# Where attention's keys and queries lie on chip, and the queue of the first queries

## The chip, the cores and the metric

The kernel runs on one core of one Trainium2 chip, as a single program. The metric is the device time of one execution in microseconds (us), taken as the median over several executions. A core has a matrix engine (PE, with its weight loads shown apart as PEld), a vector engine (DVE), an activation engine (ACT), a general engine (POOL) and a sequencer for transfers (SP). Transfers between the large memory and the on-chip memory are issued by SP, ACT or POOL, each through a queue of its own, and all of them are carried by the same 16 DMA engines.

## The reference, cut to what matters

One step of a hybrid decoder layer, for a prompt of 2,048 tokens with 16 learned tokens in front (2,064 rows) and for 8 short samples of 4 tokens:

```python
q, k, v, u = project(rmsnorm(x), w_in)          # q, k, v: 4 heads of 128; u: 512 channels
att  = head_norm(diff_attention(q, k, v))       # two softmax maps a head, one taken from the other, causal
ssm  = glu(gelu(state_space_scan(u)))           # GLU: g * sigmoid(g @ w_glu + b)
x    = x + concat([att, ssm]) @ w_out
x    = x + w_down(gelu(conv3(rmsnorm(x) @ w_gate)) * (rmsnorm(x) @ w_up))
```

The samples attend to a paged cache of 2,048 past keys and values each, which the kernel gathers page by page.

## The kernel before, in words

The work is written stage by stage in `run`. A scheduler then orders the instructions of every engine by priority (the order of the text) and by the times of its own model of the chip; inside one engine the order is fixed from then on, and each instruction waits there for what it needs. On-chip buffers come from pools. A pool has tags, a tag has so many slots of equal size, and pools opened with `side="right"` are stacked downward from the top of the on-chip memory in the order in which they are opened. When a pool is closed its bytes can be taken by a later pool, and a tile of the later pool then waits for the last use of every earlier tile whose bytes it shares, and for nothing else (`reuse_waits="tile"`). A tile that a transfer reads counts as used until that transfer has ended.

The stages around the change, and what each holds on the right-hand side (bytes per partition, counted down from the top; sizes are summed from the tile shapes in the code):

- The state space layer. `ssc` (0 to 21,056) and `ssw` (21,056 to 83,328) hold its parameters and work tiles.
- The GLU (`glu`, L1077 and on) comes after it, in eight rounds. `glc` (0 to 16,416) holds its weights. `glw` (16,416 to 63,648) holds, from the far end: two small tiles to 61,088; `ghl` for the high part (61,088 to 56,224) and `ghl` for the low part (56,224 to 51,360), one buffer each; two `gT` (51,360 to 40,608); `gh` and `gl`, two each (40,608 to 19,104); two `sg` (19,104 to 16,416). A round loads `gT` from GT, splits it into `gh` and `gl`, multiplies with the weights, forms `sg` (L1112, L1113), splits that into `ghl` (L74, L75), and SP stores both `ghl` to the tensor ST (L1123).
- The projections of keys, queries and values (`project_kvq`) run beside the GLU. The transposed keys go to KST (L367, from SP), the queries to QST (L378, from ACT), both out of the tile `khl`; the values go to VST (L323, from ACT). The last chunk of tokens does keys, then queries, then values. The pool of these tiles is on the left-hand side and ends 84,864 below the top; its second `khl` buffer is the last thing in it.
- Attention (`attend`). For each of two halves of the queries and each head, `attend_head` loads two key tiles `kt` (c = 0 and 1, L431), value tiles `vt` (L435) and `v0` (L440). For each pair of query tiles (a group, numbered 3, 2, 1, 0, -1 in the first half), `attend_queries` loads `qs` by four transfers (L450), `attend_scores` multiplies, and `attend_values` sums the values. The first head's two key loads go through POOL's queue, all others and all query loads through SP's.

Attention's four pools are `atk` (four `kt` of 8,256 and three `qs` of 4,096: 45,312), `atw` (38,848: `vt`, `v0`, `e2`, `o2`, the small sums, `wT`, `oT`), `atc` (768) and `atp` (60,928: the weights `p`). Before, they are opened in the order `atk`, `atw`, `atc`, `atp`, so `atk` lies at 0 to 45,312, with the `kt` slots at its far end (slot 0 at 45,312 to 37,056, slot 3 at 20,544 to 12,288) and the `qs` slots at the very top.

After attention `out_attention` joins its result into x, and the samples' attention starts beside it. The pools of the latter are stacked from the top again: `smc` (0 to 6,784: page table `pgt`, the indices `idx` for the gathers, small constants) and `smw` (6,784 to 55,424: among them `qbd` at 47,104 to 38,400 and the gathered rows `kv` at 38,400 to 26,112). The page table is loaded (L596), 16 small DVE instructions make `idx` (L601, L602), and POOL gathers cache rows with them (L622), after it has cleared `qbd` (L633).

Of the kernel before, what the change touches and what calls it, by code (L numbers as in the profile page):

```python
# [10 lines left out]
F32 = mybir.dt.float32  # L11
# [49 lines left out]
class Step:  # L61
# [381 lines left out]
        o2 = wp.tile([P, NM + 1024], F32, name="o2", tag="o2", bufs=2)  # L443
        return {"h": h, "half": half, "e2": e2, "o2": o2, "q0": NM + 1024 if half else 0, "kt": kt, "vc": vc, "v0": v0}

    def load_queries(self, qs, h, q0, q1):

        for dup in range(2):
            for s in range(2):
                self.nc.sync.dma_start(out=qs[dup * 64 : dup * 64 + 64, s, :, : q1 - q0].bitcast(F32),  # L450
                                       in_=self.QST[s, h, :, :, q0:q1].rearrange("c d t -> d c t"))

    def attend_queries(self, grp, wp):
        h, g = grp["h"], grp["g"]
        q0 = NM + 256 * g if g >= 0 else 0
        q1 = NM + 256 * (g + 1)
        grp["q0"], grp["q1"] = q0, q1
        qs = grp["qs"] = wp.tile([P, 2, 2, 256], F32R, name="qs", tag="qs", bufs=QB)
        self.load_queries(qs, h, q0, q1)

    def attend_scores(self, grp, qi, wp, vp, ps):

# [1170 lines left out]
    def run(self):  # L1633
        tc = self.tc

        def pool(name, bufs, **kw):
            return tc.tile_pool(name=name, bufs=bufs, reuse_waits="tile", **kw)

        with ExitStack() as st:
            e = st.enter_context  # L1640
            cp = e(pool("const", 1))
            dp = e(tc.tile_pool(name="dram", bufs=1, space=DRAM))
            self.constants(cp)
            self.scratch(dp)
            with pool("psb", 2, space=PSUM) as pb:
                with ExitStack() as right:
                    with ExitStack() as left:
                        e = left.enter_context
                        pm = e(pool("pjm", 4, space=PSUM))
                        upa = ExitStack()  # L1650
                        pa = upa.enter_context(pool("psa", 2, space=PSUM))
                        xp = e(pool("xp", 1))
                        xq = e(pool("xq", 3))
                        wq = e(pool("pjw", 9))
                        sst = ExitStack()
                        sc = sst.enter_context(pool("ssc", 1, side="right"))

                        def params():
                            with pool("ssp", 1, side="right") as sp:
                                self.ssm_params(sc, sp, pb)  # L1660
                            with pool("ctmp", 1, side="right") as tp:
                                self.constants_later(tp)

                        with pool("pu", 2) as wu:
                            self.project_setup(xp, wu, pa)
                            kept = self.project_u(xq, wq, wu, pm, pa, params)
                        with pool("cvs", 1, side="right") as sp:
                            self.conv_setup(cp, sp, pb)
                        upa.close()
                        pa, pc = e(pool("psc", 1, space=PSUM)), e(pool("psd", 1, space=PSUM))  # L1670
                        wp = e(pool("pj", 2))
                        sw = sst.enter_context(pool("ssw", 1, side="right"))
                        self.first = self.tc.cur_priority
                        mats = [self.ssm_prepare(0, sw, pb)]
                        for bk in range(8):
                            Hh = self.ssm_states(bk, mats[bk], sw, pb)
                            if bk < 7:
                                mats.append(self.ssm_prepare(bk + 1, sw, pb))
                            self.ssm_outputs(bk, mats[bk], Hh, sw, pc)
                        self.ssm_finish(sw, pb)  # L1680
                        sst.close()
                        with pool("glc", 1, side="right") as gc, pool("glw", 2, side="right") as gw:
                            self.glu(gc, gw, pb)
                        self.project_kvq(kept, xq, wp, wq, pm, pa)
            with ExitStack() as fill:
                with ExitStack() as att:
                    e = att.enter_context
                    fil = e(pool("fil", 1, space=PSUM))
                    ps = e(pool("ats", 1, space=PSUM, side="right"))
                    pools = [e(pool(nm, n, side="right")) for nm, n in (("atk", 4), ("atw", 2), ("atc", 1), ("atp", 7))]  # L1690
                    self.attend(pools, ps)
                    with pool("osc", 1) as oc, pool("osw", 2) as ow:
                        self.out_ssm(oc, ow, fil)
                    oc = fill.enter_context(pool("oac", 1))
                    with pool("oaw", 1) as ow:
                        self.out_setup(oc, ow, 1)
                        self.out_attention(range(6), ow, fil)
                up = ExitStack()
                e = up.enter_context
                pb = e(pool("psf", 4, space=PSUM, side="right"))  # L1700
                sam = ExitStack()
                sc, sw = [sam.enter_context(pool(nm, n, side="right")) for nm, n in (("smc", 1), ("smw", 2))]
                with pool("oax", 2) as ow, pool("oap", 4, space=PSUM, side="right") as pa:
                    self.out_attention(range(6, 16), ow, pa, ahead=True)
            pg = up.enter_context(pool("fg", 4, space=PSUM, side="right"))
            fx, self.fr, self.fw, self.fz = [up.enter_context(pool(nm, 1)) for nm in ("fx", "fr", "fw", "fz")]
            self.up_setup(fx, pg, pb)
            self.sample_attention(sc, sw, pb)
            sam.close()
            with pool("obc", 1, side="right") as oc, pool("obw", 1, side="right") as ow:  # L1710
                self.out_setup(oc, ow, 2)
                self.out_attention([16], ow, pb)
            with pool("dw", 1, side="right") as wp:
                self.ffn_up()
                up.close()
                with pool("du", 1, side="right") as du, pool("dps", 1, space=PSUM) as pd, pool("da", 1) as da:
                    self.ffn_down(wp, da, du, pd)
# [59 lines left out]
```

## Time and profile before

| | us |
|---|---|
| median of 3 executions | 2915.77 |
| lowest, highest | 2908.78, 2924.84 |
| the profiled execution | 2908.63 |
| its span on the core | 2906.9 |
| PE busy | 2731.3 (94% of the span) |
| DVE busy | 2181.1 (75%) |
| ACT busy | 1505.3 (52%) |
| POOL busy | 830.7 (29%) |
| DMA, mean rate over the span | 176 GB/s |

The profile is of one execution. Busy time is the sum of an engine's instructions; idle time before an instruction carries the name of what ended it, and only idle time of the engine that sets the end costs anything. The granted clock of PE is given as a share of its full speed of 2.4 GHz (0.50 is its lower level, 1.2 GHz). A wait on several things is put down to the one that ended last by the profile, so the name can be that of something which merely ended near that moment.

### The profile page before, as it was taken

The page shows a single profiled execution, that of the slowest core. Times are in us where ns is not written, and L with a number is a line of the kernel's source. Part 1 is how long each engine was busy: PE and PEld are TensorE (multiplying, and loading weights), DVE is VectorE, ACT ScalarE, POOL GpSimd, SP SyncE. Part 2 cuts the span into 40 slices and gives each one's busy share as a digit, 9 for nine tenths or more (in the row PEclk, how much of TensorE's full clock was granted, in tenths as well). Part 3 has the DMA queues.
Part 4 walks back from the last instruction along what each step waited for, and adds up shares of the span by engine and source line. Part 5 has one row for each costly group of instructions (what it writes and reads, how often), then busy time and mean ns, then how long its engine had stood idle before and what let it go on. Part 6 is the DMA issues. An engine that isn't in the chain of part 4 may idle for free. (4 is left out here: it accounts for less than half of the span.)

```text
span 2906.9 us, 43475 instructions
## 1 busy us (share of the span) xinstructions
PE 2731.3 (94%) x14872; PEld 2359.9 (81%) x14872; DVE 2181.1 (75%) x4318; ACT 1505.3 (52%) x3051; POOL 830.7 (29%) x1272
## 2 busy tenths in 40 slices
PE   6899889989999999788999999999999999999999
PEld 6866668868887878667988998988998998787786
DVE  6748977756677888457888788888788995675565
ACT  5423334556667888236566556655555663222233
POOL 2525442112211232554343332342213442000000
PEclk9899999999999999899999999999999999999999
DMA  6676676787664442686455546454454437675562
GB/s 187 174 184 151 176 197 175 200 241 195 215 193 135 139 129 64 202 279 197 155 169 175 167 151 207 151 174 155 141 186 127 132 119 282 201 239 192 178 224 91
DMA packets 434614, 512.13 MB, mean 176 GB/s; under 512 B 91337, under 2 KB 339033, under 8 KB 433368
## 3 DMA queue, kind: packets, MB, share of 16 engines
q1 hardware_dynamic: 336520, 347.45, 41.6%
q0 software_dynamic: 23296, 82.81, 8.9%
q10 hardware_dynamic: 74576, 79.09, 8.2%
q8 instruction: 117, 1.92, 0.3%
q14 instruction: 105, 0.86, 0.1%
HBM read 381.32 MB, written 126.74 MB: 175 GB/s over the span
## 5 line engine op out<-in xcount | busy, mean ns | idle before, releaser
L80 PE MATMUL g<-xb,uw 128*128 128x384 f32 (+1 forms) x1848 | 596.3, 325 | 13.0 <-ACT uw L68 5.8
L81 PE MATMUL g<-xb,uw 128*128 128x384 f32 (+1 forms) x1848 | 595.3, 323 | 0.0
L82 PE MATMUL g<-xb,uw 128*128 128x384 f32 (+1 forms) x1848 | 583.0, 323 | 2.2 <-DVE uw L69 2.2
L80 PEld LDWEIGHTS g<-xb,uw 128*128 128x128 f32 x1848 | 347.6, 188 | 25.5 <-ACT uw L68 7.0
L81 PEld LDWEIGHTS g<-xb,uw 128*128 128x128 f32 x1848 | 348.1, 188 | 7.9 <-issue 2.3
L82 PEld LDWEIGHTS g<-xb,uw 128*128 128x128 f32 x1848 | 345.0, 188 | 9.3 <-DVE uw L69 3.5
L68 ACT ACTIVATE uw<-uraw 128x512 fp32r<-128x512 f32 x330 | 200.7, 625 | 122.3 <-PE g L82 74.5
L69 DVE TENSOR_TENSOR uw<-uraw,uw 128x512 fp32r<-128x512 f32 x330 | 241.6, 739 | 27.0 <-ACT uw L68 25.0
L491 ACT ACTIVATE p<-S,nms 128x484 f32<-128x484 f32 (+11 forms) x360 | 209.3, 590 | 63.3 <-DVE nms L490 50.5
L490 DVE TENSOR_REDUCE nms<-S 128x1 f32<-128x484 f32 (+11 forms) x360 | 191.5, 559 | 50.0 <-PE S L485 27.0
L80 PE MATMUL pq<-dw,da 128*128 128x512 f32 x528 | 209.7, 398 | 11.0 <-ACT da L68 7.3
L81 PE MATMUL pq<-dw,da 128*128 128x512 f32 x528 | 209.5, 397 | 0.0
L82 PE MATMUL pq<-dw,da 128*128 128x512 f32 x528 | 200.4, 395 | 6.2 <-DVE da L69 6.2
L68 ACT ACTIVATE da<-dt 128x1024 fp32r<-128x1024 f32 (+1 forms) x68 | 71.2, 1047 | 215.2 <-PE pq L82 146.6
L80 PE MATMUL pj<-wh,x 128*128 128x512 f32 (+1 forms) x408 | 168.7, 416 | 13.1 <-DVE wk L337 5.5
L81 PE MATMUL pj<-wl,x 128*128 128x512 f32 (+1 forms) x408 | 168.8, 414 | 3.8 <-DVE wl L75 3.8
L95 POOL TENSOR_TENSOR rs_y<-rs_v,half 128x8 f32<-128x8 f32 (+4 forms) x77 | 93.3, 1216 | 269.4 <-DVE rs_v L90 251.5
L82 PE MATMUL pj<-wh,x 128*128 128x512 f32 (+1 forms) x408 | 167.5, 411 | 0.0
L1322 POOL TENSOR_TENSOR uraw<-uraw 128x512 f32<-128x512 f32 x66 | 107.6, 1631 | 176.6 <-DVE s L1320 109.0
L484 PE MATMUL S<-kt,qs 128*128 128x484 f32 (+11 forms) x360 | 143.6, 401 | 8.4 <-DMA qs<-QST 5.3
L552 PE MATMUL O<-wT,vt 128*128 128x256 f32 x576 | 145.0, 388 | 2.6 <-ACT wT L547 2.1
L1449 DVE SCALAR_TENSOR_TENSOR z<-A,cw,z 128x768 f32<-128x768 f32 (+1 forms) x132 | 136.6, 1035 | 4.9 <-ACT z L1446 4.0
(434 smaller groups left out, 6867.4 us busy)
## 6 DMA issues: line engine op xcount, KB each, us to landing
dt<-MT SPq DMA_DIRECT2D x99, 512.0 KB
uraw<-in_w_gate_dram SPq DMA_DIRECT2D x66, 512.0 KB
uraw<-in_w_up_dram SPq DMA_DIRECT2D x66, 512.0 KB
raw<-in_w_in_dram SPq DMA_DIRECT2D x80, 256.0 KB
MT<-z ACTq DMA_DIRECT2D x44, 384.0 KB
qs<-QST SPq DMA_DIRECT2D x128, 128.0 KB
dT<-in_w_down_dram SPq DMA_DIRECT2D x44, 256.0 KB
draw<-in_w_down_dram POOLq DMA_DIRECT2D x44, 256.0 KB, 4.2
```

The lines of the kernel that those rows point to most:

```text
L68: nc.scalar.activation(hi, src, AF.Copy)
L69: nc.vector.tensor_tensor(out=lo, in0=src, in1=hi.bitcast(F32), op=ALU.subtract)
L80: mm(out, lhsT=lh, rhs=rh, start=start, stop=False, skip_group_check=goes_on)
L81: mm(out, lhsT=lh, rhs=rl, start=False, stop=False, skip_group_check=goes_on)
L82: mm(out, lhsT=ll, rhs=rh, start=False, stop=stop, skip_group_check=goes_on)
L95: nc.gpsimd.tensor_tensor(out=y, in0=v, in1=e, op=ALU.pow)
L484: nc.tensor.matmul(dst, lhsT=qs[:, 0, c, qa : qa + M], rhs=kt[c][:, x:y], start=True, stop=False)
L490: nc.vector.tensor_reduce(out=nms[:M, z : z + 1], in_=dst, axis=AX.X, op=ALU.max, negate=True)
L491: nc.scalar.activation(p[:M, Z + x : Z + y], dst, AF.Exp, bias=nms[:M, z : z + 1], accum_out=sms[:M, z : z + 1])
L552: nc.tensor.matmul(O[:, :N], lhsT=v, rhs=tw[:, m - a, :N], start=(m == 0), stop=(m == nb))
L1322: gp.tensor_tensor(out=a21, in0=a11, in1=a21, op=ALU.subtract)
L1449: nc.vector.scalar_tensor_tensor(out=z[:, :np_], in0=A[:, j : j + np_], scalar=cw[:, f, j : j + 1], in1=z[:, :np_], op0=ALU.mult, op1=ALU.add)
```

## The change

The pool with the keys and queries is opened third instead of first, so the four pools lie in the order `atw`, `atc`, `atk`, `atp`. Summed as above, `atw` is then at 0 to 38,848, `atc` at 38,848 to 39,616, and `atk` at 39,616 to 84,928: `qs` slots 2, 1, 0 at 39,616 to 43,712, 47,808 and 51,904, then `kt` slots 3, 2, 1, 0 at 51,904 to 60,160, 68,416, 76,672 and 84,928. `atp` stays where it was. Besides, the four query loads of head 0, group 3 (the first group of all) are issued by POOL instead of SP.

```diff
-    def load_queries(self, qs, h, q0, q1):
+    def load_queries(self, qs, h, q0, q1, eng):
         for dup in range(2):
             for s in range(2):
-                self.nc.sync.dma_start(out=qs[dup * 64 : dup * 64 + 64, s, :, : q1 - q0].bitcast(F32),
-                                       in_=self.QST[s, h, :, :, q0:q1].rearrange("c d t -> d c t"))
+                eng.dma_start(out=qs[dup * 64 : dup * 64 + 64, s, :, : q1 - q0].bitcast(F32),
+                              in_=self.QST[s, h, :, :, q0:q1].rearrange("c d t -> d c t"))
...
-        self.load_queries(qs, h, q0, q1)
+        self.load_queries(qs, h, q0, q1, self.nc.gpsimd if (h, g) == (0, 3) else self.nc.sync)
...
-                    pools = [e(pool(nm, n, side="right")) for nm, n in (("atk", 4), ("atw", 2), ("atc", 1), ("atp", 7))]
-                    self.attend(pools, ps)
+                    wp, cp_, kp, vp = [e(pool(nm, n, side="right")) for nm, n in (("atw", 2), ("atc", 1), ("atk", 4), ("atp", 7))]
+                    self.attend((kp, wp, cp_, vp), ps)
```

## Rows read from the trace of the kernel before

**Rows 1.** The page's first part: busy time, share of the span, instructions.
```profile
PE 2731.3 (94%) x14872; PEld 2359.9 (81%) x14872; DVE 2181.1 (75%) x4318; ACT 1505.3 (52%) x3051; POOL 830.7 (29%) x1272
```
**Rows 2.** Stretches: length, busy PE, PEld, DVE, ACT, POOL, clock, DMA share, GB/s.
```profile
624.00:664.00 40.00, 28.03 (x108) 19.42 (x107) 18.20 (x57) 20.48 (x58) 5.44 (x32) 0.79 1.08 290
636.00:640.00 4.00, 4.00 (x12) 2.63 (x12) 1.94 (x4) 2.47 (x6) 0.00 (x0) 0.55 1.03 289
654.00:664.00 10.00, 8.73 (x26) 6.34 (x27) 4.14 (x15) 4.50 (x13) 1.47 (x8) 0.52 1.14 237
...
1160.00:1200.00 40.00, 27.34 (x134) 22.50 (x133) 18.78 (x52) 14.56 (x36) 17.63 (x21) 0.79 0.53 147
1200.00:1350.00 150.00, 119.45 (x581) 98.53 (x579) 91.88 (x145) 62.83 (x113) 81.09 (x83) 0.92 0.83 263
1350.00:2425.00 1075.00, 1059.43 (x6451) 992.71 (x6452) 935.98 (x1534) 632.78 (x1102) 367.58 (x419) 1.00 0.50 156
```
**Rows 3.** PE in time order: start, length, instruction, idle before it and its releaser.
```profile
635.79 1.86 PE L484 MATMUL S<-kt,qs 128*128 128x456 f32 x4 [5.27 <-DMA qs<-QST]
...
654.84 0.77 PE L80 MATMUL po<-owh,sa 128*128 128x512 f32 x1 [3.98 <-DMA sa<-ST]
```
**Rows 4.** SP's issues in time order around the end of the projections.
```profile
608.54 2.73 SPq L1123 DMA_DIRECT2D ST<-ghl  x2
...
623.87 0.36 SPq L1123 DMA_DIRECT2D ST<-ghl  x1
...
627.63 2.45 SPq L450 DMA_DIRECT2D qs<-QST  x3
...
631.61 0.58 SPq L450 DMA_DIRECT2D qs<-QST  x1
```
**Rows 5.** POOL's issues of the first two key tiles.
```profile
622.85 0.75 POOL L431 DMA_DIRECT2D kt<-KST  x1 [20.57 <-DMA VST<-v]
624.40 0.54 POOL L431 DMA_DIRECT2D kt<-KST  x1 [0.79 <-DVE ghl L75]
```
**Rows 6.** Waits of SP's queue, 600 to 680 us: in total, times, longest.
```profile
SPq L1123 <- DMA QST<-khl: 8.0, 1, 8.0
...
SPq L450 <- DMA ST<-ghl: 0.9, 1, 0.9
```
**Rows 7.** ACT's issues of the last query stores.
```profile
616.81 1.92 ACTq L378 DMA_DIRECT2D QST<-khl  x3
...
618.81 0.60 ACTq L378 DMA_DIRECT2D QST<-khl  x1
```
**Rows 8.** Issue to landing of POOL's two key loads, by the view of that tile.
```profile
DMA to landing us min/median/max: 6.0/6.8/7.6
```
**Rows 9.** POOL's weight loads late in the kernel (line L1504), and their landing.
```profile
L1504 POOL DMA_DIRECT2D draw<-in_w_down_dram x44: 536/536/538, 2440.0 to 2818.4; - x44
...
DMA to landing us min/median/max: 2.7/5.4/9.5
```
**Rows 10.** DVE in time order near attention's end.
```profile
1165.29 1.26 DVE L601 TENSOR_SCALAR idx<-pgt 128x8 int32<-128x8 int32 x2 [0.99 <-issue]
1166.46 0.68 DVE L549 COPY wT<-tpw 128x512 f32<-128x512 f32 x1
1167.06 1.88 DVE L601 TENSOR_SCALAR idx<-pgt 128x8 int32<-128x8 int32 x3
```
**Rows 11.** PE in the same stretch.
```profile
1167.19 1.12 PE L545 MATMUL tpw<-ident,p 128*128 128x128 f32 x4 [3.63 <-DVE wT L549]
...
1185.36 1.56 PE L552 MATMUL O<-wT,vt 128*128 128x256 f32 x6 [0.58 <-ACT wT L547]
```
**Rows 12.** SP's issues at attention's end.
```profile
1162.67 0.39 SPq L596 DMA_DIRECT2D pgt<-in_page_rows_dram  x1
...
1197.40 0.29 SPq L582 DMA_DIRECT2D RR<-rr  x1
```
**Rows 13.** POOL at attention's end.
```profile
1195.30 1.01 POOL L633 MEMSET qbd<- 128x1088 f32 x1
1196.48 1.13 POOL L622 DMA_INDIRECT kv<-in_cache_k_dram,idx  x1 [0.17 <-issue]
```

## The prediction

> **What bounds the kernel now.** I read the page's first part first: PE is busy for 94% of the span [rows 1], so the time moves only where PE stands still, or runs at its lower clock. The second view is the table of stretches [rows 2]. The FFN stretch, 1350 to 2425 us, has 1059 of 1075 us of PE busy at full clock, and the change does not touch it. Two stretches near the change have holes. The first is the seam between the projections and attention, 624 to 664 us: PE is busy 28.0 of 40 us at a mean clock of 0.79, while the DMA engines are full (share 1.08, 290 GB/s). The second is attention's end and what follows, 1160 to 1350 us: 12.7 of 40 and 30.6 of 150 us are idle.
>
> PE's own order [rows 3] names the two holes of the seam. The first scores start at 635.79 us, 5.27 us after the last projection, and the wait ended with a query load. The second stop, 3.98 us, ended at 654.84 us with a load of the stored GLU output for the output projection (`sa`). After each stop PE ran at about half clock: 4.0 us of work at 0.55 and 8.73 us at 0.52 [rows 2].
>
> Why the queries were late stands in SP's queue [rows 4, 6]. It stands at its own stores of the GLU's result: after the pair at 608.54 it waited 8.0 us for a query store and then for the GLU's last round, whose second store of ST went out at 623.87. Value loads came next. Three query loads were issued from 627.63 to 630.08, and the fourth at 631.61, held in its last 0.9 us by that last ST store. So the store issued at 623.87 landed at about 631.6.
>
> **The change part by part.**
>
> The four query loads leave SP. They take 2.45 + 0.58 = 3.0 us of SP's queue [rows 4], and what stands behind them, the queries of group 2, moves up by that. PE waits for none of these later, so I count nothing; what hides it is the work of the first group. If that cover went, up to 3.0 us could be won.
>
> POOL gets them. The first key load was issued at 622.85 and the second at 624.40, 0.75 and 0.54 us each [rows 5]. The question is what they and the queries now wait for, and that is read from bytes and from one row. The second key load waited for the GLU's last `ghl` split [rows 5]. That split reads `sg`, which lay at 19,104 to 16,416 from the top, and of the four old key slots only slot 3 (20,544 to 12,288) shares bytes with it. So the two first keys sit in slots 0 and 3, and I take it that the first queries, like the first keys, sit in slot 0. In the new places:
> - Key slot 0 (84,928 to 76,672) lies under the state space layer, but its last 64 bytes are those of the projection's second `khl` buffer, which ends at 84,864. Whether the last queries used that buffer no row says; I take it so. Its last store was issued from 618.81 to 619.41 [rows 7]. The first of those four, issued from 616.81, ended SP's 8.0 us wait at 608.54 + 2.73 + 8.0 = 619.3 [rows 4, 6, 7], so one takes about 2.5 us, and the load may go at about 621.9 instead of 622.85. Keys were not what PE waited for: nothing gained.
> - Key slot 3 (60,160 to 51,904) lies under both `ghl`, and query slot 0 (51,904 to 47,808) shares 544 bytes with the second. Both must wait until the last ST store has landed. That is the same store that held the fourth query load, but now it holds all four, and a key load before them.
>
> When does it land? No row has it under the new load. Not before 624.2 + 2.5 = 626.7 (the query store's time), not after the old 631.6. I take 629.8, near the late end, because the DMA engines stay full: only the 520 KB of the second key tile move behind it, 1.8 us at 290 GB/s [rows 2]. Then POOL issues one key and four query loads, 0.54 to 0.75 us each [rows 5]: 3.2 us, to 633.0. Landing: POOL's key loads took 6.0 to 7.6 us [rows 8], its loads in a calmer place 2.7 to 9.5, median 5.4 [rows 9], the fourth query load on SP about 3.6 (632.2 to 635.79) [rows 3, 4]. I take 5.0, between the last two, as these loads are as small as those. The first scores then start at 638.0, 2.2 us later than before. The ends are 626.7 + 2.7 + 2.7 = 632.1 (3.7 earlier) and 631.6 + 3.75 + 7.6 = 643.0 (7.2 later).
>
> How much of that reaches the end? The next stop, the 3.98 us before 654.84, ends with data that come through the full DMA engines, and the change takes no byte away. A later start of the scores eats into that stop. I count 1.0 of the 2.2 us as lost.
>
> The rows on the queue itself: on SP the fourth load stood from 630.08 to 631.61 [rows 4], so another queue could be worth 1.5 us if the slot did not bring the same wait back. The Trainium skill, "DMA: Bandwidth & Descriptors", section "Issuing engines are not separate DMA queues", says that loads issued by different engines run on the same 16 DMA engines and that a second issuer saves only the time to initiate them. By that rule the move gives PE nothing; by the row it would take 1.5 us off the sum.
>
> The value side (`atw`) moves to the top, over the GLU's buffers, free by the GLU's last products; its loads were behind SP's stores anyway: nothing.
>
> At attention's end the samples' small tiles (`smc`, 0 to 6,784) lay over query slots, and the page table was loaded right after the last scores, at 1162.67 [rows 12]. Now they lie over `wT` and `oT`, which the last value products read, until 1185.36 + 1.56 = 1186.9 [rows 11]. Two effects:
> - The `idx` instructions leave the middle of attention's tail. DVE stood 0.99 us for the table and worked 1.26 us on `idx` just before the copy at 1166.46 [rows 10] for which PE waited 3.63 us [rows 11]. That is 2.2 us won; between 0, if something else ends that wait, and 4.1, with the 1.88 us that follow [rows 10].
> - The gathers, which began at 1196.48 [rows 13], may come later. The table lands 2.6 us after issue (1162.67 to 1165.29) [rows 10, 12], so at 1189.5; 16 `idx` instructions at no more than 3.14 / 5 = 0.63 us [rows 10] end by 1199.5. And `qbd` (47,104 to 38,400) now shares bytes with `atc`, whose last row store is issued at 1197.40 [rows 12] and lands by about 1200.0, where the clearing of `qbd` started at 1195.30 [rows 13]. Standing behind it on POOL are the gathers: they would go at 1201.2, 4.7 us late. Or POOL takes them first and loses nothing. I take 1.0, nearer to nothing, since DVE has little else to do there.
>
> Sum: +1.0 - 2.2 + 1.0 = -0.2 us on the profiled execution's 2908.6, so 2908.4. That execution is 7.1 us under the median of 2915.8, and I put the forecast beside the median: 2915.6. The scheduler will also reorder what follows by its own model. The 43.2 us of idle PE from 1160 to 1350 [rows 2] are what it can gain from or add to; I allow a sixth, 7 us, either way.
>
> **The rivals.**
>
> *The title comes true (faster).* The keys and queries used first lie only under the state space layer, because slots are given out otherwise than I read. Then all is loaded while the projections still run, and the seam loses both stops and both stretches at half clock: 5.27 + 3.98 + 4.0 x 0.45 + 8.73 x 0.48 = 15.2 us, 2900.6. For it: the 5.27 us wait did end with a query load. Against it: the 64, 544 and 8,256 bytes shared, and a second stop that the DMA engines set. If only the first stop goes, with its slow stretch, it is 7.1 us: 2908.7, inside half a per cent.
>
> *The gathers slide (slower).* The place is POOL's queue at attention's end, the price the slide of the first gather. The page table itself is 24.2 us later (1162.67 to 1186.9). If the scheduler sees it late, it puts POOL's work for the next output tiles ahead, and the gathers, which feed PE's filling work until 1350, start that much later. It decides from a first gather after 1196.5 + 14.6 = 1211.1; half way to the full slide it is about 19 us: 2935. For it: DMA is at 0.83 in that stretch [rows 2], so lost gather time is hard to make up. Against it: before, 33.8 us lay between the table's load and the first gather [rows 12, 13], of which table and `idx` needed 12.6.
>
> *The first scores late at the seam (slower, small).* The upper end of the landing: 7.2 us, 2923, if the second stop absorbs nothing.
>
> **How the numbers follow.** Half a per cent, 14.6 us, is about what a measurement of this kernel can tell from no change; three executions spread over 16 us. My forecast with its bounds and the small cases on both sides stays within it: 0.81. The first rival in full is the only way to more than that on the fast side: 0.10. The sliding gathers: 0.09. The range goes from 2900, which just takes in the fast rival, to 2915.8 + 7.2 + 4.7, about 2928; the sliding gathers stay outside.
>
> **What would show it.** Right: POOL's second key load and the four query loads stand until an ST store has landed, at 627 to 632 us; PE's wait before the first scores is 3 to 10 us and ends with a query or key load; no `idx` instruction runs before the last value products. Wrong: query loads on POOL before 623 us and scores that follow the projections at once; or a first gather after 1211 us, with PE idle for more than 45 us from 1160 to 1350.

## The result, and the profile after

The changed kernel took 2930.06 us (median of 11 executions, 2926.39 to 2937.28), the kernel before 2915.77 on the same chip: it is slower by 14.3 us between the medians. The ratio of the two sets of runs, with its 95% interval, is 1.0068 (1.0055 to 1.0081), which would be 20 us. Here and below a ratio is taken over all runs of both kernels; it is not the quotient of the two medians, which is 1.0049 here. The loss is outside the range that was given, and on the side that had a chance of 0.09. The profiled execution after has a span of 2927.3 us, 20.4 more than before, and the shares of the loss below are those of these two executions.

The page's first part, as in [rows 1]:

```profile
PE 2727.7 (93%) x14872; PEld 2356.9 (81%) x14872; DVE 2174.6 (74%) x4318; ACT 1502.3 (51%) x3051; POOL 849.6 (29%) x1276
```

The work is the same (only POOL has four more instructions, the query loads), so the loss is idle time of PE. These are the stretches of the changed kernel, with the same columns as [rows 2], and under them the one stretch of the kernel before that those rows do not have:

```profile
624.00:664.00 40.00, 15.10 (x47) 10.03 (x45) 5.11 (x6) 4.37 (x5) 3.49 (x8) 0.62 1.01 282
630.00:700.00 70.00, 40.45 (x190) 31.20 (x190) 31.03 (x88) 31.51 (x89) 10.02 (x44) 0.73 0.73 206
1160.00:1200.00 40.00, 34.32 (x199) 28.69 (x200) 25.89 (x76) 26.88 (x75) 6.53 (x22) 1.00 0.23 71
1200.00:1350.00 150.00, 110.92 (x531) 90.71 (x529) 75.57 (x142) 50.31 (x92) 79.31 (x78) 0.87 0.77 239
1350.00:2425.00 1075.00, 1059.05 (x6406) 990.89 (x6407) 938.15 (x1523) 637.18 (x1109) 384.20 (x420) 1.00 0.51 159
```

```profile
630.00:700.00 70.00, 57.62 (x280) 44.24 (x279) 44.90 (x139) 48.33 (x145) 13.20 (x67) 0.88 0.89 239
```

Between 630 and 700 us PE is busy 40.45 us instead of 57.62. The last projection ends at 630.5 in both, so these 17.2 us are lost at the seam, and they are most of the 20.4. The FFN stretch has not changed. What PE does at the seam now, in time order (idle time before an instruction and its releaser in brackets):

```profile
648.76 0.77 PE L80 MATMUL po<-owh,sa 128*128 128x512 f32 x1 [18.31 <-DMA sa<-ST]
...
658.15 0.80 PE L80 MATMUL po<-owh,sa 128*128 128x512 f32 x1 [5.92 <-ACT owh L68]
...
660.43 1.72 PE L485 MATMUL S<-kt,qs 128*128 128x456 f32 x4
...
667.19 0.54 PE L80 MATMUL po<-owh,sa 128*128 128x512 f32 x1 [3.14 <-ACT owh L68]
```

Before, the first thing after the projections was a score matmul and `po`, the output projection of the state space half, came 19 us later [rows 3]. Now nine `po` matmuls stand in PE's program ahead of the first scores, which start at 660.43 and waited for no load of their own: PE's order is a different one. SP and ACT have been reordered in the same sense:

```profile
631.56 1.33 SPq L435 DMA_DIRECT2D vt<-VST  x2
633.66 1.92 SPq L1133 DMA_DIRECT2D oraw<-in_w_out_dram  x2
636.60 2.46 SPq L1153 DMA_DIRECT2D sa<-ST  x2
...
648.64 0.33 SPq L431 DMA_DIRECT2D kt<-KST  x1
650.13 10.54 SPq L450 DMA_DIRECT2D qs<-QST  x8
```

```profile
645.59 1.06 ACT L68 ACTIVATE owh<-oraw 128x1024 fp32r<-128x1024 f32 x1 [14.51 <-DMA oraw<-in_w_out_dram]
647.31 1.06 ACT L68 ACTIVATE owh<-oraw 128x1024 fp32r<-128x1024 f32 x1 [0.66 <-DMA oraw<-in_w_out_dram]
657.04 1.06 ACT L68 ACTIVATE owh<-oraw 128x1024 fp32r<-128x1024 f32 x1 [8.68 <-DMA oraw<-in_w_out_dram]
666.08 1.06 ACT L68 ACTIVATE owh<-oraw 128x1024 fp32r<-128x1024 f32 x1 [7.98 <-DMA oraw<-in_w_out_dram]
667.15 1.28 ACT L492 ACT_TABLE_LOAD   x1
```

SP loads output weights (`oraw`) and `sa` first and the queries of the next two groups (eight loads) only from 650.13. Before, these eight followed the first group's last load at once:

```profile
631.61 8.04 SPq L450 DMA_DIRECT2D qs<-QST  x9
```

ACT's four splits of output weights stand ahead of the first exponentials. ACT is idle for 31.8 us in all before them, each time until weights have landed, and is through with them at 667. Both engines work through their lists in order, so attention stands behind loads that it does not need.

The steps that were read from shared bytes can be seen on POOL, and the landing of the queries in the view of transfers:

```profile
622.04 0.75 POOL L431 DMA_DIRECT2D kt<-KST  x1 [18.84 <-DVE sg L1114]
632.28 0.54 POOL L431 DMA_DIRECT2D kt<-KST  x1 [9.49 <-DMA v<-VST]
632.82 2.42 POOL L450 DMA_DIRECT2D qs<-QST  x4
```

```profile
qs<-QST POOLq DMA_DIRECT2D x4, 128.0 KB, 8.3
```

The first key load goes at 622.04 and the second stands until 632.28. By the shared bytes the wait there is for the last stores of ST; the profile names a value load that ended near that moment (in the kernel with the place alone, below, it names a store of ST). The four query loads follow and are there about 8.3 us after issue, by 643.5. PE does not ask for them before 660. At attention's end:

```profile
1201.46 1.56 PE L553 MATMUL O<-wT,vt 128*128 128x256 f32 x6 [0.58 <-ACT wT L548]
```

```profile
1211.28 0.24 DVE L602 TENSOR_SCALAR idx<-pgt 128x8 int32<-128x8 int32 x2
```

```profile
1213.56 1.00 POOL L634 MEMSET qbd<- 128x1088 f32 x1 [0.68 <-DMA RR<-rr]
1214.73 1.14 POOL L623 DMA_INDIRECT kv<-in_cache_k_dram,idx  x1 [0.17 <-DVE idx L602]
```

No `idx` runs before the last value products any more. Those end at 1203.0 instead of 1186.9 [rows 11], and the first gather is 18.25 us later than before [rows 13], of which 16.1 were lost earlier: the slide at this place is 2.1 us. In the 179.1 us behind the last value product PE is busy 137.4 us, against 141.2 before, so the rest of the 20.4 us, about 4, is lost there. Whether that belongs to the change or to these two executions, one profile of each does not say; three kernels with the same place at attention's end lose nothing in all (below).

### The profile page after: what moved, and what is told of

Its sections match the earlier page's. It is cut to its first block, busy times and chain, and to the rows that moved or that the text cites. A ratio compares the mean times of both kernels' runs of the same rounds, so it can differ in the third digit from the quotient of the medians.

```text
span 2927.3 us, 43472 instructions
## 1 busy us (share of the span) xinstructions
PE 2727.7 (93%) x14872; PEld 2356.9 (81%) x14872; DVE 2174.6 (74%) x4318; ACT 1502.3 (51%) x3051; POOL 849.6 (29%) x1276
```

## The experiments

The table sums them up; each ratio is against the kernel before on the same chip, with its 95% interval. "Behind" is the time from the end of the last projection to the first scores (0: no idle time between), each from one profile of that kernel.

| kernel | first in the program after the projections | behind, us | ratio |
|---|---|---|---|
| before | scores | 5.3 | 1 |
| after | `po` | 30.0 | 1.0068 (1.0055 to 1.0081) |
| place only | `po` | 26.3 | 1.0090 (1.0067 to 1.0112) |
| queue only | scores | 5.0 | 0.9990 (0.9977 to 1.0003) |
| after, PE's scores first | scores on PE, splits on ACT | 9.5 | 1.0096 (1.0073 to 1.0119) |
| after, keys' pool 704 B up | scores | 9.3 | 0.9993 (0.9977 to 1.0008) |
| after, keys' pool 80 B up | scores | 10.0 | 1.0003 (0.9991 to 1.0016) |
| after, tiles clear, pool not | `po` | 27.6 | 1.0101 (1.0084 to 1.0119) |
| after, splits later | scores, but weights first on SP | 9.6 | 1.0051 (1.0033 to 1.0069) |
| after, splits and loads later | scores | 9.5 | 1.0004 (0.9988 to 1.0020) |
| all clear | scores | 0 | 0.9978 (0.9961 to 0.9995) |
| all clear, queries by SP | scores | 2.4 | 1.0010 (0.9996 to 1.0024) |
| all clear, behind the last GT | scores | 0 | 0.9999 (0.9984 to 1.0013) |
| the same, weights sooner | scores | 0 | 1.0004 (0.9991 to 1.0018) |

**The two halves of the change, one at a time.** First the place without the queue:

```diff
-        self.load_queries(qs, h, q0, q1, self.nc.gpsimd if (h, g) == (0, 3) else self.nc.sync)
+        self.load_queries(qs, h, q0, q1, self.nc.sync)
```

> The placement of the change alone: the first queries go by SP again, the pools stay as the change has them. Theory A (the place made TensorE's program put nine matmuls of the output projection, po, ahead of the first scores, and on the chip their operands come late, 17 us of idle at 630 to 700): the order is the same, first scores at 655 to 663 us, 2926 to 2932 us. Theory B (the place lets the gathers at attention's end slide, which is most of the loss): also 2926 to 2932. Theory C (POOL's queue brings the first queries late, 8.3 us of landing against 3.6 by SP): 2914 to 2918, since the queue is undone.

Then the queue without the place:

```diff
-                    wp, cp_, kp, vp = [e(pool(nm, n, side="right")) for nm, n in (("atw", 2), ("atc", 1), ("atk", 4), ("atp", 7))]
-                    self.attend((kp, wp, cp_, vp), ps)
+                    pools = [e(pool(nm, n, side="right")) for nm, n in (("atk", 4), ("atw", 2), ("atc", 1), ("atp", 7))]
+                    self.attend(pools, ps)
```

> The queue alone: the first queries by POOL, the pools placed as before the change. A: TensorE's program has scores first, so no nine po matmuls; first scores within 5 us of 635.8, 2913 to 2919 us. B: 2913 to 2919, as the place is undone. C: first scores 4 to 8 us later than 635.8 and 2920 to 2928.

The place alone gives 2928.53 us, 1.0090, with the nine `po` in front (first scores at 652.12, the last projection having ended at 625.82 in that execution). The queue alone gives 0.9990. So the loss is all the place's, and theory C is out. Its premise came true all the same: by POOL the four loads were all issued by 622.8, ahead of the end of the projections at 625.5, but took 8.7 us to land, and the first scores came 5.0 us behind the projections, as before. What the earlier issue won, the longer landing took.

**TensorE's order alone put right.** The matmuls of the first output projection are queued behind a score matmul, on PE and nowhere else:

```diff
-                nc.tensor.matmul(dst, lhsT=qs[:, 0, c, qa : qa + M], rhs=kt[c][:, x:y], start=True, stop=False)
+                s = nc.tensor.matmul(dst, lhsT=qs[:, 0, c, qa : qa + M], rhs=kt[c][:, x:y], start=True, stop=False)
+                if self.s0 is None and qi == 6:
+                    self.s0 = s
...
-                    with pool("osc", 1) as oc, pool("osw", 2) as ow:
+                    with pool("osc", 1) as oc, pool("osw", 2) as ow, self.tc.issue_after(self.s0.ins):
                         self.out_ssm(oc, ow, fil)
```

> The changed kernel with the matmuls of the first output projection held in TensorE's program behind the first scores of the seventh query tile (about where they stand in the kernel before); pools and queue as in the change. A: first scores at 643 to 647, when the queries of 632.8 + 8.3 us are there, idle of TensorE from 630 to 700 at 17 to 22 us instead of 29.6 (12.4 before), 2917 to 2924 us. B: the seam gains what A says but the end stays 4 to 7 us late, so it would be 2926 or more only if B is most of the loss. C: first scores no earlier than 650 and 2926 or more.

It gave 1.0096: nothing was won. PE in that kernel, in time order:

```profile
637.25 1.86 PE L486 MATMUL S<-kt,qs 128*128 128x456 f32 x4 [9.50 <-DMA qs<-QST]
...
662.51 0.66 PE L486 MATMUL S<-kt,qs 128*128 128x346 f32 x1 [21.51 <-ACT p L495]
```

The first scores come at 637.25, somewhat sooner than theory A had them (643 to 647), and then PE stands 21.51 us for the exponentials, because ACT's list still has the four splits in front. Theory A was too narrow: it is not PE's order but the order on all engines that changed, and putting one right only moves the stop.

**Where the order comes from.** The projections' pool and the pool `atk` share 64 bytes (`khl` ends 84,864 below the top, `atk` at 84,928). The next kernel puts the pool `atc` below `atk`:

```diff
-                    wp, cp_, kp, vp = [e(pool(nm, n, side="right")) for nm, n in (("atw", 2), ("atc", 1), ("atk", 4), ("atp", 7))]
+                    wp, kp, cp_, vp = [e(pool(nm, n, side="right")) for nm, n in (("atw", 2), ("atk", 4), ("atc", 1), ("atp", 7))]
```

> The changed kernel with the 768 B pool of attention's small row sums taken from above the keys' pool and put below it: the keys' pool then begins 704 B above the pool of the projections (it shared 64 B with it), the second key tile still shares bytes with the gated layer's outputs. A, with the 64 shared bytes as the reason for the order: TensorE's program has scores first; first scores at 638 to 644, idle of 630 to 700 at 12 to 18 us, 2914 to 2921 us. B: 2926 or more, the place at attention's end is unchanged. C: 2922 or more, the queries still come by POOL.

2903.99 us against 2906.04, 0.9993. The second key tile still shares bytes with the outputs of the GLU (its load stood until 627.10), and attention's end still has the new place; with the 64 bytes no longer shared, the order and the time are those of before. A sharper form of it, 80 bytes in place of 768:

```diff
-            nms = wp.tile([P, 5], F32, name="nms", tag="nms", bufs=12)
+            nms = wp.tile([P, 5], F32, name="nms", tag="nms", bufs=8)
```

> The changed kernel with 8 instead of 12 buffers for the 20 B tiles of row maxima, which stand above the keys' pool: the pool then begins 80 B higher, 16 B above the end of the projections' pool, and nothing else moves but by 80 B. Theory P (the 64 bytes that the keys' pool shared with the projections' pool decide the order in which the program is laid out, and that order is the loss): scores and exponentials first, as before the change, ratio to before 0.997 to 1.002. Theory D (it was the 768 B pool that the earlier run moved, or another size): ratio 1.006 to 1.010 as for the changed kernel.

1.0003. PE's first scores there:

```profile
637.95 1.86 PE L485 MATMUL S<-kt,qs 128*128 128x456 f32 x4 [10.01 <-DMA qs<-QST]
```

The counterpart: the key tiles and queries lie clear of every earlier tile, but the pool as a whole still has its foot in the shared bytes, with another tile (`oT`) on them that is written much later:

```diff
-            kt.append(kp.tile([P, TP], F32R, name="kt", tag="kt", bufs=4))
+            kt.append(kp.tile([P, TP], F32R, name="kt", tag="k" + "ab"[h % 2], bufs=2))
...
+        self.kp, self.oT0 = kp, kp.tile([P, 2 * P], F32, name="oT", tag="oT", bufs=2)
...
-        oT = wp.tile([P, 2 * P], F32, name="oT", tag="oT", bufs=2)
+        oT, self.oT0 = self.oT0, None
+        if oT is None:
+            oT = self.kp.tile([P, 2 * P], F32, name="oT", tag="oT", bufs=2)
```

> The changed kernel with the first key tiles and queries lying clear of every buffer of the projections and of the gated layer (key tiles in two tags, and above two tiles of attention's outputs, which now stand at the pool's foot): no key or query load waits for anything at the seam, as in the clear layout that ran at 0.998, but the pool as a whole still shares its lowest 64 bytes with the projections' pool. Theory P1 (the sharing of the pools decides the program's order, whichever tile lies in the shared bytes): TensorE's program has nine po matmuls ahead of the first scores again, ScalarE's splits of the output weights ahead of the first exponentials, ratio 1.005 to 1.010. Theory P2 (the key tile's own 64 bytes decide): scores first, ratio 0.997 to 1.000.

1.0101, the whole loss. POOL, and PE, in time order:

```profile
614.68 1.31 POOL L432 DMA_DIRECT2D kt<-KST  x2 [0.66 <-DMA QST<-khl]
615.97 2.44 POOL L451 DMA_DIRECT2D qs<-QST  x4
```

```profile
641.63 0.77 PE L80 MATMUL po<-owh,sa 128*128 128x512 f32 x1 [16.50 <-DMA sa<-ST]
...
652.75 1.66 PE L486 MATMUL S<-kt,qs 128*128 128x456 f32 x4
```

Here keys and queries are asked for at 614.68 to 618.4, before the projections end, and yet the first scores run at 652.75, behind `po`. The waits on the chip go by tiles; the order was made when the program was laid out, and there it goes with the pools. This kernel also moves `oT`, which was not tried by itself with nothing shared; the key tiles' two tags were, below, and there the scores come first. How the scheduler's model comes to it (most simply: a pool may start only when the pool under it has been given back, after its last value stores) was not tried by itself and is argued only.

**What of the order costs how much.** In the changed kernel ACT's splits are queued behind the first exponentials of the seventh query tile, and in a second kernel, which adds one more `issue_after` to the same line, SP's loads of `oraw` and `sa` behind the second head's key loads as well. The first kernel's edit:

```diff
-                nc.scalar.activation(p[:M, Z + x : Z + y], dst, AF.Exp, bias=nms[:M, z : z + 1], accum_out=sms[:M, z : z + 1])
+                e = nc.scalar.activation(p[:M, Z + x : Z + y], dst, AF.Exp, bias=nms[:M, z : z + 1], accum_out=sms[:M, z : z + 1])
+                if self.s0 is None and qi == 6:
+                    self.s0 = e
...
-                    with pool("osc", 1) as oc, pool("osw", 2) as ow:
+                    with pool("osc", 1) as oc, pool("osw", 2) as ow, self.tc.issue_after(self.s0.ins):
                         self.out_ssm(oc, ow, fil)
```

> The changed kernel, pools and queue as it has them, with ScalarE's splits of the output weights (owh) held in its program behind the first exponentials of the seventh query tile; loads on SP stay as they are. P: TensorE's program then has scores first by itself, no wait of 21 us for ScalarE behind the first scores; SP still issues the output weights and sa ahead of the next queries (at 644 to 652), so part of the loss stays: ratio 1.000 to 1.005. If the loss sits at attention's end: 1.006 or more.

> The same, and SP's loads of the output weights and of sa held behind the load of the second head's second key tile (where SP has them before the change). P: the whole loss of the seam is gone with the shared bytes still there: ratio 0.997 to 1.002, first scores at 8 to 12 us behind the last projection. If the loss sits at attention's end or in the shared bytes' waits themselves: 1.005 or more.

Splits later: 1.0051. Both later: 1.0004, all of the loss gone with the 64 bytes still shared and the place at attention's end unchanged. So neither the waits that those bytes bring nor attention's end make up the loss; the order does. What was left after the first step is one wait of PE, for queries that SP had issued behind the weights and `sa`:

```profile
640.90 4.17 SPq L451 DMA_DIRECT2D qs<-QST  x4
```

```profile
635.65 1.86 PE L486 MATMUL S<-kt,qs 128*128 128x456 f32 x4 [9.62 <-DMA qs<-QST]
...
651.16 0.61 PE L486 MATMUL S<-kt,qs 128*128 128x328 f32 x1 [7.83 <-DMA qs<-QST]
```

**Does the idea work when nothing is shared?** The kernel with the pool 704 bytes up, and the key tiles in two tags, so that both first key tiles and the first queries lie below all of the GLU's large buffers:

```diff
-            kt.append(kp.tile([P, TP], F32R, name="kt", tag="kt", bufs=4))
+            kt.append(kp.tile([P, TP], F32R, name="kt", tag="k" + "ab"[h % 2], bufs=2))
```

> The earlier run with the keys' pool 704 B up, and the key tiles in two tags so that both first key tiles and the first queries lie below every buffer of the gated layer: no key or query load waits for its stores any more. P: what the second key tile's wait cost at the first scores (635.35, 9.3 us of idle) shrinks by 3 to 6 us but comes back at the next stop (the stores' landing for sa, the splits of the output weights): ratio 0.997 to 1.001, like the earlier run. Theory W (the waits on the gated layer's stores cost what they show): 3 to 6 us less than the earlier run, ratio 0.994 to 0.997.

2898.48 us against 2908.39, 0.9978. The scores follow the projections at once, but PE stood earlier:

```profile
606.31 0.93 PE L80 MATMUL z<-gh,gwh 128*128 128x336 f32 x2 [5.60 <-ACT gh L68]
...
630.90 0.37 PE L485 MATMUL S<-kt,qs 128*128 128x456 f32 x1
...
651.30 0.77 PE L80 MATMUL po<-owh,sa 128*128 128x512 f32 x1 [6.12 <-DMA sa<-ST]
```

The key and query loads, issued at 595.99 to 599.9, run beside the loads of the GLU's last round, whose products now wait 5.60 us, and the stop for `sa` is still there, with 6.12 us. Three more kernels start from this one. In the first the queries go by SP (the first diff above):

> The layout in which the first keys and queries lie clear of everything, with the first queries on SP again: the queue's half of the change taken away where its other half does what it says. SP then issues them behind its four stores of ST (it stood at them to 624 in the earlier run). If POOL's queue is worth its time once nothing else holds the queries: first scores 4 to 8 us behind the last projection instead of none, no stop of 5.6 us at 606, ratio 0.998 to 1.001, 0 to 3 us slower than with POOL's queue. If what the early queries cost the last GT loads is as much as they save: the same ratio as with POOL, 0.997 to 0.999.

In the second POOL's loads are held until the last GT load has landed:

```diff
+            if r == 7:
+                self.last = nc.gpsimd.tensor_copy(cp.tile([P, 1], F32, name="gdum"), gT[:, 0, CH - 1, :1])
...
-                head = self.attend_head(h, half, kp, wp)
+                if h or half:
+                    head = self.attend_head(h, half, kp, wp)
+                else:
+                    with self.tc.issue_after(self.last.ins):
+                        head = self.attend_head(h, half, kp, wp)
```

> The clear layout with POOL's key and query loads held behind the landing of the last round's GT loads (a one-element copy by POOL that reads them stands ahead of the key loads): in the earlier run they were issued at 596 to 600, and TensorE stood 5.6 us at 606 for that round. If those loads delayed GT: the stop at 606 falls to 2 us or less, the keys and queries still land before the last projection, ratio 0.995 to 0.998. If the stop has another reason: it stays, and the ratio is 0.998 as before.

In the third, besides, the first loads of `oraw` and `sa` are given the priority of the first groups' queries (shown for `sa`; the edit around the load of `oraw` is the same):

```diff
...
+            now = self.tc.cur_priority
+            if t < 2:
+                self.tc.cur_priority = self.pA
             for s in range(2):
                 nc.sync.dma_start(out=a[:, s, :, :n].bitcast(F32), in_=self.ST[s, :, :, tk].rearrange("k p t -> p k t"))
+            self.tc.cur_priority = now
```

> The same, and SP's loads of the first two output weights and of the first sa tiles ahead of its loads of the second head's keys and values (scheduling priority alone; splits and matmuls stay where they are). If the second stop (sa, 6 us in 640 to 660) waits for SP's order: idle of 640 to 680 falls by 3 to 6 us, ratio 0.993 to 0.997. If the DMA engines are the limit there (share over 1.0 from 630 to 660 in the kernel before): no more than 1 us, the ratio of the run beside it.

They gave 1.0010, 0.9999 and 1.0004. By SP the first scores came 2.4 us behind the projections, sooner than the 4 to 8 that were expected. In the second kernel the stop of 5.6 us has gone, in the third the stop for `sa` as well, and neither is faster for it. PE and ACT in the third, in time order, suggest where the time is taken back:

```profile
626.25 0.37 PE L491 MATMUL S<-kt,qs 128*128 128x456 f32 x1
...
636.63 0.66 PE L491 MATMUL S<-kt,qs 128*128 128x346 f32 x1 [7.62 <-ACT p L498]
```

```profile
626.58 0.34 ACTq L322 DMA_DIRECT2D out_dram<-v  x1
630.08 0.33 ACTq L323 DMA_DIRECT2D VST<-v  x1
632.31 0.34 ACTq L322 DMA_DIRECT2D out_dram<-v  x1
634.20 0.33 ACTq L323 DMA_DIRECT2D VST<-v  x1
634.55 1.28 ACT L498 ACT_TABLE_LOAD   x1 [7.51 <-DMA qs<-QST]
```

The scores run at 626.25, but ACT has four stores of values to issue first. They go one after another until 634.5, since in the program each of the last three waits for an earlier transfer of SP's that has nothing to do with its data (a value load and two query loads), and the first exponential is at 635.85. The second kernel has the same stop, with 6.43 us. In the first clear kernel the four stores were out by 633.6, PE's stop for the exponentials was only 2.01 us, and the ratio is 0.9978. So it looks as if early scores win nothing while those stores stand in front; a kernel with the stores moved was not run. Nor is a gain from early scores shown: the 0.9978 has an interval that stays below 1, but its two relatives with the same early scores are at 1.000.

## Why the prediction was wrong

**The step that failed** is the one on the first key tile: "its last 64 bytes are those of the projection's second `khl` buffer", and then "nothing gained", that is, nothing at all. As a wait it was read rightly (the load was put at about 621.9, and went at 622.04). But sharing those 64 bytes cost the whole loss: 80 bytes higher, and the ratio is 1.0003. I treated shared bytes as waits in a program whose order stays, while the order itself changed with them. The prediction knew that "the scheduler will also reorder what follows by its own model" and allowed 7 us for it, at attention's end. The reordering was at the seam, and cost 17.2 us there.

**The second key tile and the queries** (+2.2 us at the first scores, 1.0 of it lost) stood up where the order stayed. The reading of bytes was right: the load stood until 632.28, against 629.8 taken, 0.7 us past the late end of 631.6. The landing was put too low: 5.0 us were taken, with 7.6 as the late end, and it took 8.3 in the changed kernel and 6.0 and 6.3 in the two kernels with the pool higher up. In the kernel 80 bytes up, the first scores came 10.0 us behind the projections instead of 5.3, so 4.7 us later, within the bound of 7.2; the time did not change. The stop for `sa` of 3.98 us [rows 3] is not there any more in its profile, which fits the sum's view that a later start eats into that stop. In the changed kernel itself this term is never seen, as PE runs `po` first.

**The queue.** Nothing was given for it, and 1.5 us by SP's row. Alone it made 0.9990 with 1 inside its interval, which does not tell the two apart. The Trainium skill, "DMA: Bandwidth & Descriptors", section "Issuing engines are not separate DMA queues", says that transfers started by different engines run on the same 16 DMA engines, and that starting them from several saves only the time to initiate them. That ratio does not speak against it. In the layout where nothing is shared, 0.9978 by POOL and 1.0010 by SP lean the other way, but they are from two sets of runs and their intervals all but touch, so this stays open.

**Attention's end** (-2.2 and +1.0). That no `idx` runs before the last value products came true, and the gathers slid by 2.1 us, within the 4.7 allowed. The 2.2 us were not won: the stop of 3.63 us behind `idx` is gone, but PE now stands 1.64 and 2.09 us for `wT` in the same tail, so it was the case in which something else ends that wait. Three kernels with this place and the old order at the seam are at 0.9993, 1.0003 and 1.0004, so the end costs or gives less than can be measured. The sign that was named for the rival of the sliding gathers, a first gather after 1211, came (1214.73) for another reason: a fixed time cannot tell a slide from a delay that came earlier. That its price, 2935, lies near the 2930.06 that came is chance: the place was another. The other half of that sign, over 45 us of idle PE from 1160 to 1350, just did not (44.8 by the rows above).

**The rivals.** The first, that all is loaded while the projections run, was built, and its three forms with POOL's queue lie at 0.9978 to 1.0004, so it is worth 6 us at the most seen (11 by the end of that interval), not 15.2. The second stop did not go with the first: in two of the three forms PE still stands for `sa` (6.12 and 4.12 us), and in two it stands for the exponentials behind ACT's stores (6.43 and 7.62 us). The rival that was missing: the output projection goes ahead of attention at the seam, at a price of some 17 us, as soon as the two pools share bytes, if only 64.

## What to carry to other kernels

Where a scheduler lays out the program, a new place for a buffer can also be a new order: before costing the waits that shared bytes bring, look which pools touch each other, also by a few bytes, and count a reordering of all engines' lists as a case of its own, priced by the stage that would be passed over. If a profile shows an engine idle at the start of a stage, look whether the work that it runs first there is the same as before, and then at every engine's list: with the matmuls' order put right alone, the wait moved to ACT and nothing was won. An early arrival of data is worth no more than the gap to the next stop; here first scores 5 us earlier or later than before changed the time by 0.2% at most.

## What the runs showed that was not expected

64 shared bytes of a stack of 145,856 moved the time by 0.7 to 1.0%, and where the keys and queries lay clear (1.0101) no load of theirs waited for these bytes at all. And the issue of a transfer can hold an engine long after its own data are ready: ACT's four value stores took from 626.58 to 634.53, 0.33 to 0.34 us each, and the rest went by while, in the program, they stood for transfers of SP's.
